# Three more output weights stored as halves in the tail of the first feed-forward, six units of the second set read from there

## The chip, the cores and the metric

The kernel runs on one core of one Trainium2 chip. The metric is the device time of one execution in microseconds. The kernel before takes 2192.62 us (median of 3 runs, 2192.11 to 2194.38). Five engines work side by side, each through its own instructions in a fixed order: PE (TensorE, matmuls), DVE (VectorE), ACT (ScalarE), POOL (GpSimd), and SP (SyncE), which here only issues DMAs.

## The reference

It is one inference step of a two-layer encoder trunk over 1056 tokens (1024 of a prompt and 32 of a sample) and 1024 channels, in float32. The part that the change touches is the second layer's attention and what frames it:

```
# layer 0: mLSTM mixer, then feed-forward;  layer 1: windowed attention, then feed-forward
x = layer_norm(ALPHA * x + mixer(x))
x = layer_norm(ALPHA * x + swiglu(x, w_gu[0], w_down[0]))          # first feed-forward
kv = x @ w_kv
q  = x @ w_q_b
o  = sink_attention(q, k, v, sinks, alibi)                         # 16 heads of 64
x  = layer_norm(ALPHA * x + o @ w_out_b)                           # w_out_b: 1024 x 1024
x  = layer_norm(ALPHA * x + swiglu(x, w_gu[1], w_down[1]))
```

## The kernel before

Activations lie transposed in SBUF: 8 tiles of 128 channels by 1056 tokens. The tokens are worked in quarters of 264 columns (in the projections for attention in groups of 384, 384 and 288). Every float32 product is made of three matmuls (`gemm`, L435 to L437): each operand is split in a high half `hi`, rounded to the format that the matmul takes, and a low half `lo = x - hi`; the three are hi·hi, hi·lo and lo·hi.

So each weight has to be split before use. A *unit* is a block of 128 output channels by 1024 input channels, and it is split in two *halves* f = 0 and 1 of 128 x 512 each. The class `Weights` does it in the order of use: SP loads the raw unit (512 KB) in a buffer `wr` (four of them), ACT (or POOL) casts it to `wh`, DVE or POOL subtracts to `wl` (L256 to L260). Five pairs `wh`/`wl` rotate, and some halves have a *home* of their own in memory that lies free at that time (`oh`, and `ex` of the next stage).

Some units are split ahead of time. While PE is busy with the first feed-forward, the task `split_before` loads half a unit at a time (`wraw`), casts it on ACT (`whi`, L1335), subtracts on DVE (L1337) and stores both results in a DRAM tensor `halves` (L1340). `BEFORE` lists these units: 2 of w_kv, 8 of w_q_b, and the first 3 (`EARLY`) of w_out_b, 26 halves in all. When `Weights` comes to such a unit, SP loads two blocks of 256 KB from `halves` (L253) in place of the raw load, cast and subtraction.

w_out_b is walked twice. The first set of its 8 units (118, 121, 124 and 125 to 129 in the program's count) makes the first quarter of columns, while attention still runs. The second set, units 130 to 137, makes quarters two to four, where each unit stays in memory until its third use. In the kernel before all of 130 to 137 are loaded raw and split on ACT and DVE; 132 to 137 go to homes in `ex`, memory that the attention's tiles leave free. When the first quarter is done, `finish` waits for the attention's last pieces, and the layer norm of each quarter (`ln_task`) runs on DVE, ACT and a few PE matmuls (L496, L513) beside the next quarter's matmuls.

Between attention and this product stands `mixed_parts`: it splits the attention's output (ACT, and DVE or POOL, L465 and L466) and then has SP load the residual input back from DRAM into the same place (`act<-scrx`, L1248). SP takes all DMAs in the order in which they were written, and so a DMA that waits holds those behind it.

The tail of the first feed-forward (`norm_tail` with `run`, L1657 on) multiplies its last eight weights (`dnt`) with the four quarters; the adds to `act` (L1662) are on DVE, with the layer norm of the quarter before.

Of the kernel before, what the change touches and what calls it, by code (L numbers as in the profile page):

```python
# [18 lines left out]
KT = D // P  # L19
# [10 lines left out]
LC = 64  # L30
WK = 3 * LC
EARLY = 3
D_FF = 2816
FT = D_FF // P

# [269 lines left out]
def kernel(ctx: ExitStack, tc: tile.TileContext, A, O):  # L305
    nc = tc.nc
    ctx.enter_context(tc.manual_schedule())
    wv = Weave()
# [3 lines left out]
    def pool(name, space=None, side=None):  # L312
        kw = {}
        if space is not None:
            kw["space"] = space
        if side is not None:
            kw["side"] = side
        return tc.tile_pool(name=name, bufs=1, reuse_waits="tile", **kw)

    def new(p, tag, shape, dt=F32, bufs=1):  # L320
        uid[0] += 1
        return p.tile(list(shape), dt, name=f"{tag}_{uid[0]}", tag=tag, bufs=bufs)
# [6 lines left out]
    units, on_vector, pairs = [], set(), set()  # L329

    def add(name, idx):
        units.append(A[name][idx] if idx is not None else A[name])
        return len(units) - 1
# [34 lines left out]
    U_KV, U_QB, U_OUT_B = [], [[], []], [[], []]  # L368
# [3 lines left out]
    for jp in range(QH // 4):  # L372
        U_QB[1] += [add("wqb", 2 * jp + i) for i in range(2)]
        if 0 < jp <= EARLY:
            U_OUT_B[0].append(add("wout_b", jp - 1))
    U_OUT_B[0] += [add("wout_b", u) for u in range(EARLY, 8)]
    U_OUT_B[1] += [add("wout_b", u) for u in range(8)]
# [1 line left out]
    on_vector.update((u, f) for u in U_O + U_OUT_A[0] for f in range(2))  # L379
    on_vector.update((u, f) for u in U_OUT_B[1][2:] for f in range(2))  # L380
    on_vector.update((u, f) for u in U_Q[:1] for f in range(2))
    on_vector.update((u, f) for u in U_OUT_B[1][:2] for f in range(2))
    on_vector.update((u, 0) for u in U_OUT_B[0][EARLY:])
    W = Weights(nc, base, units, pairs, on_vector, {(u, 1) for u in U_OUT_B[0][EARLY:]})
    BEFORE = [("wkv", i) for i in range(2)] + [("wqb", i) for i in range(8)] + [("wout_b", i) for i in range(EARLY)]
    for us in (*U_KV, *U_QB, U_OUT_B[0][:EARLY]):
        name = {2: "wkv", 8: "wqb", EARLY: "wout_b"}[len(us)]
        W.ready.update((u, BEFORE.index((name, i))) for i, u in enumerate(us))
    W.early = {up[i] for up in U_UP for i in range(FIRST, FT)}
    wv.feed = W.feed  # L390
# [23 lines left out]
    scr = dram.tile([P, KT, T], F32, name="scrx")  # L414
    W.halves = dram.tile([P, len(BEFORE), 2, 2, D // 2], F32, name="halves")
    OPS = ("x11", "x21", "t2", "t4", "t1", "t3", "x22")
# [136 lines left out]
    class LastNorm:  # L553
# [36 lines left out]
        def run(self):  # L590
            acc, sq = self.buf(0, 2), [self.buf(2 + 2 * i, 2) for i in range(3)]
            yield 1.2
            self.pc = self.bank()
            nc.tensor.matmul(self.pc, onesm[:], self.buf(10), start=True, stop=True)
            yield 0.6
            self.centre(3)
            self.centre(4, 2)
            self.centre(6, 2)
            self.centred = True
            yield 0.6  # L600
            self.centre(0, 2)
            nc.scalar.activation(sq[0], self.z(0, 2), AF.Square)
            self.centre(2)
            while self.i < 3:
                yield 0.3
            yield 0.6
            nc.scalar.activation(sq[1], self.z(2, 2), AF.Square)
            nc.gpsimd.tensor_add(acc, self.z(0, 2), self.z(2, 2))
            yield 1.0
            nc.vector.tensor_add(sq[0], sq[0], sq[1])  # L610
            while self.i < 5:
                yield 0.3
            yield 0.6
            nc.scalar.activation(sq[1], self.z(4, 2), AF.Square)
            nc.vector.tensor_add(acc, acc, self.z(4, 2))
            nc.vector.tensor_add(acc[:, 0], acc[:, 0], acc[:, 1])
            yield 1.4
            nc.vector.tensor_add(sq[0], sq[0], sq[1])
            nc.vector.tensor_add(sq[0][:, 0], sq[0][:, 0], sq[0][:, 1])
            while self.i < 6:  # L620
                yield 0.3
            nc.scalar.activation(sq[2][:, 0], self.z(6), AF.Square)
# [42 lines left out]
    def norm_tail(li, run, box, final=False):  # L665


        tasks = []
        for g, (cols, (c, zs)) in enumerate(QUARTERS):

            def after(order, i):
                if i in (3, 5, 7):
                    if i == 3 and g > 1:
                        wv.drain(tasks[g - 2])
                    acc = box[0].z[:, 0:2, c, zs]
                    pair = [ACT[:, order[j] : order[j] + 2, cols] for j in (i - 1, 0)]
                    nc.vector.tensor_add(acc, acc if i > 3 else pair[1], pair[0])
                if i == KT - 1:
                    nc.vector.tensor_add(acc[:, 0], acc[:, 0], acc[:, 1])

            if final and g == 3:
                wv.drain(tasks[1])
                run(g, cols, None, LastNorm(box[0].z, box[0].lnps, QUARTERS[g], li))
                break
            run(g, cols, after)
            if g == 0 and li & 1:
                nc.scalar.preload_act_table_set("natural_log_exp_and_others")
            last = g >= 3
            tasks.append(wv.launch(ln_task(box[0].z, box[0].lnps, QUARTERS[g], li, last, final)))
            box[0].norms = tasks  # L690
        return tasks
# [582 lines left out]
    def mixer_out(us, li, lx, opening=None, before=None, made=0):  # L1274

        box = [lx]

        def run(g, cols, after):
            if before:
                before(g)  # L1280
            if g == 3:
                lx = box[0]
                lx.sums = ExitStack()
                su = lx.sums.enter_context(pool("sums"))
                bufs = [new(su, f"su{i}", [P, 2, N4])[:] for i in range(2)]
                wv.drain(lx.norms[1])
                lx.comb = wv.launch(sums(lx, li, 0, bufs, 2.4))

            order = [6, 7, *range(6)] if g == 3 and not opening else list(range(KT))
            for i, m in enumerate(order):  # L1290
                if not g and m < made:
                    continue
                u = us[g > 0][m]
                W.get(u)
                if g < 2:
                    W.split_to(us[g][min(m + 2, KT - 1)])
                out_tile(u, m, cols)
                if g == 3 or u not in us[1]:
                    W.done(u)
                if g == 3 and (u, 0) in W.home:  # L1300
                    box[0].left += 1
                if box[0]:
                    after(order, i)
            if not box[0]:
                box[0] = opening()
                for i in range(KT):
                    after(order, i)

        return norm_tail(li, run, box), box[0]

    def split_before():

        ex = ExitStack()
        p = ex.enter_context(pool("before"))
        raws = [new(p, f"wraw{i}", [P, D // 2]) for i in range(2)]
        hi = new(p, "whi", [P, D // 2], F32R)
        todo = [(i, f) for i in range(len(BEFORE)) for f in range(2)]  # L1320

        def load(n):
            i, f = todo[n]
            name, idx = BEFORE[i]
            nc.sync.dma_start(raws[n % 2][:], A[name][idx][:, f * (D // 2) : (f + 1) * (D // 2)])

        load(0)
        yield 4.0
        for n, (i, f) in enumerate(todo):
            yield 3.0  # L1330
            if n + 1 < len(todo):
                load(n + 1)
            yield 2.0
            r = raws[n % 2][:]
            nc.scalar.copy(hi[:], r)  # L1335
            yield 1.5
            nc.vector.tensor_sub(r.bitcast(F32R), r, hi[:].bitcast(F32))  # L1337
            yield 1.8
            for k, t in enumerate((hi[:].bitcast(F32), r)):
                nc.sync.dma_start(W.halves[:, i, f, k, :], t)  # L1340
            W.stored.add((i, f))
            yield 3.7
        ex.close()

    def ffn(layer, li, tasks, lx, final):
# [26 lines left out]
        staging, splitting = [], []  # L1372
# [260 lines left out]
        for b in range(TAIL):  # L1633
# [8 lines left out]
            for j in range(2):  # L1642
                down(b, j)
            wv.drain(feeding.pop())
        for t in splitting:
            wv.drain(t)
        px.close()
        W.ahead = True
        dense_psum(5)
# [15 lines left out]
                    W.done(u)  # L1665

        r = norm_tail(li, run, [lx], final)
        lx.ex.close()
        return r

# [18 lines left out]
    n = D // 2  # L1689
# [353 lines left out]
    def before(g):  # L2043
        if g == 0:
            wv.drain(task, lambda: ast["placed"] >= last_item(7, 0))
        if g < 3:
            parts_made(g)
# [170 lines left out]
```

## Time and profile before

| | |
|---|---|
| runs | 2192.11, 2192.62, 2194.38 us |
| profiled execution, its own time | 2192.83 us |
| its span, first to last instruction | 2190.7 us |
| granted TensorE clock | 0.998 |
| PE busy | 2162.7 us (99%) |
| DVE, ACT, POOL busy | 1455.3, 991.9, 903.3 us |
| DMA | 322 MB, mean 147 GB/s |

What follows goes by microseconds from the span's start. The first feed-forward's tail is at about 1094 to 1164, attention with its projections at 1164 to 1406, the second set of output weights at 1406 to 1500. PE's busy time counts a matmul from its start to a modelled end, so that it says nearly always 99%; idle time is read from the waits and from the distance of one matmul's start to the next.

### The profile page before, as it was taken

What the parts mean: (1) busy time and instruction counts of PE and PEld (TensorE: products, weight loads), DVE (VectorE), ACT (ScalarE), POOL (GpSimd) and SP (SyncE); (2) the same over time, 40 slices, a digit from 0 to 9 for tenths busy, and PEclk for the clock granted to TensorE, in tenths of its full rate; (3) what the DMA queues carried; (4) which work ended last, traced back from release to release, by engine and by line L of the source; (5) the groups of instructions that cost most, each with busy time, mean ns of one, the idle gap of its engine ahead of it and who ended that gap; (6) DMA issues with size and microseconds to landing.
All of it is one profiled execution on the core that took longest, in us unless ns stands there. A gap on an engine that the chain in (4) does not pass through costs nothing.

```text
span 2190.7 us, 44028 instructions
## 1 busy us (share of the span) xinstructions
PE 2162.7 (99%) x16982; PEld 2136.5 (98%) x16982; DVE 1455.3 (66%) x2833; ACT 991.9 (45%) x2234; POOL 903.3 (41%) x926
## 2 busy tenths in 40 slices
PE   9999999999999999999999999999999999999997
PEld 9999999999999999999999999999999999999997
DVE  4465676778767666466657776888666666457657
ACT  4443355455444444322235777656444444422125
POOL 2544210003655655454421443501665655554441
PEclk9999999999999999999999999999999999999999
DMA  5221112212656555697517433511443433397712
GB/s 172 75 66 55 51 49 80 96 40 69 235 197 208 211 201 200 205 333 252 180 45 245 150 118 126 161 35 39 145 146 143 158 140 143 131 358 244 254 52 80
DMA packets 187361, 322.49 MB, mean 147 GB/s; under 512 B 18768, under 2 KB 124296, under 8 KB 187152
## 3 DMA queue, kind: packets, MB, share of 16 engines
q1 hardware_dynamic: 182800, 315.36, 43.1%
q10 hardware_dynamic: 4352, 4.33, 0.6%
q8 instruction: 134, 2.20, 0.4%
q14 instruction: 75, 0.61, 0.1%
HBM read 221.23 MB, written 96.57 MB: 145 GB/s over the span
## 4 chain that ended last, share of the span: by engine, by line
PE 86%; DVE 7%; ACT 3%; issue 1%; DMA 1%; POOL 0%; SPq 0%; DVEq 0%; ACTq 0%; POOLq 0%
PE d L435 10%; PE A L435 10%; PE A L437 10%; PE A L436 10%; PE d L437 10%; PE d L436 10%; PE B L435 7%; PE B L436 7%; PE B L437 7%; PE O L1986 1%; PE psS L1898 1%; PE T L1957 1%; DMA hs_x<-z 1%; ACT act L538 1%; PE T L988 1%
## 5 line engine op out<-in xcount | busy, mean ns | idle before, releaser
L260 POOL TENSOR_TENSOR wl_s<-wr,wh_s 128x512 fp32r<-128x512 f32 x224 | 304.2, 1367 | 241.2 <-ACT wh_s L258 181.4
L435 PE MATMUL d<-sx,wh 128*128 128x264 f32 (+2 forms) x1040 | 331.4, 319 | 0.2
L260 POOL TENSOR_TENSOR wl_a<-wr,wh_a 128x512 fp32r<-128x512 f32 x112 | 155.7, 1392 | 401.9 <-ACT wh_a L258 397.7
L437 PE MATMUL d<-sx,wl 128*128 128x264 f32 (+2 forms) x1040 | 316.2, 304 | 1.7 <-DVE wl L260 0.9
L436 PE MATMUL d<-sx,wh 128*128 128x264 f32 (+2 forms) x1040 | 315.7, 304 | 0.6 <-DVE sx L466 0.4
L435 PE MATMUL A<-sx,wh_s 128*128 128x264 f32 x896 | 254.5, 284 | 0.0
L436 PE MATMUL A<-sx,wh_s 128*128 128x264 f32 x896 | 254.2, 284 | 0.0
L437 PE MATMUL A<-sx,wl_s 128*128 128x264 f32 x896 | 254.0, 284 | 0.0
L258 ACT CAST wh_s<-wr 128x512 fp32r<-128x512 f32 x224 | 135.7, 618 | 192.1 <-DVE wr L201 102.9
L435 PEld LDWEIGHTS d<-sx,wh 128*128 128x128 f32 x1040 | 196.0, 188 | 3.6 <-ACT sx L465 0.4
L436 PEld LDWEIGHTS d<-sx,wh 128*128 128x128 f32 x1040 | 196.3, 189 | 1.9 <-DVE sx L466 1.1
L437 PEld LDWEIGHTS d<-sx,wl 128*128 128x128 f32 x1040 | 195.5, 188 | 2.4 <-DVE wl L260 1.4
L435 PE MATMUL d<-sx,ex 128*128 128x264 f32 x624 | 180.7, 290 | 0.1
L436 PE MATMUL d<-sx,ex 128*128 128x264 f32 x624 | 177.2, 284 | 0.0
L437 PE MATMUL d<-sx,ex 128*128 128x264 f32 x624 | 176.9, 284 | 0.0
L437 PEld LDWEIGHTS A<-sx,wl_s 128*128 128x128 f32 x896 | 168.8, 188 | 0.0
L435 PEld LDWEIGHTS A<-sx,wh_s 128*128 128x128 f32 x896 | 168.4, 188 | 0.2 <-issue 0.2
L436 PEld LDWEIGHTS A<-sx,wh_s 128*128 128x128 f32 x896 | 168.4, 188 | 0.0
L1396 POOL TENSOR_TENSOR z<-z 128x528 fp32r<-128x528 f32 x76 | 103.9, 1367 | 122.6 <-ACT z L1395 114.1
L435 PE MATMUL A<-ex,wh_s 128*128 128x264 f32 x448 | 127.5, 285 | 0.0
L436 PE MATMUL A<-ex,wh_s 128*128 128x264 f32 x448 | 127.1, 284 | 0.0
L437 PE MATMUL A<-ex,wl_s 128*128 128x264 f32 x448 | 127.1, 284 | 0.0
(377 smaller groups left out, 7126.6 us busy)
## 6 DMA issues: line engine op xcount, KB each, us to landing
wr<-in_gu SPq DMA_DIRECT2D x92, 512.0 KB, 4.4
hs_x<-z SPq DMA_DIRECT2D x72, 528.0 KB, 3.1
hs_t<-z SPq DMA_DIRECT2D x64, 528.0 KB, 4.7
sx<-hs_x SPq DMA_DIRECT2D x112, 264.0 KB, 5.9
sx<-hs_t SPq DMA_DIRECT2D x64, 264.0 KB, 6.1
ex<-hs_t SPq DMA_DIRECT2D x64, 264.0 KB, 6.0
wr<-in_dn SPq DMA_DIRECT2D x32, 512.0 KB, 4.9
wh<-halves SPq DMA_DIRECT2D x38, 256.0 KB, 3.2
```

What stands on the lines that cost most here:

```text
L258: self.nc.scalar.copy(hi, r)
L260: eng.tensor_sub(lo, r, hi.bitcast(F32))
L435: nc.tensor.matmul(out, ah, bh, start=start and k == 0, stop=False, **kw)
L436: nc.tensor.matmul(out, ah, bl, start=False, stop=False, **kw)
L437: nc.tensor.matmul(out, al, bh, start=False, stop=stop and k == last, **kw)
L538: nc.scalar.activation(z, z, AF.Identity, scale=gk, bias=bk)
L988: nc.tensor.matmul(pc[:, : 2 * (DV + 1)], keys, vt[j][:, c], start=True, stop=True)
L1396: eng.tensor_sub(lo.bitcast(F32R), buf(s), hi)
L1898: nc.tensor.matmul(ps[:rows, at : at + nk], lhs, k[:, k0 : k0 + nk], start=i == 0, stop=i == 1)
L1957: nc.tensor.transpose(pt[:nk, t, :rows], p[:rows, at : at + nk], ident[:rows, :rows])
L1986: nc.tensor.matmul(out, v[:nk], x, start=i == 0, stop=i == len(todo) - 1)
```

## The change

The list `BEFORE` grows by three units, so that w_out_b's units 0 to 5 are stored (32 halves in all). The first 26 halves are made when they were. The last six wait until the tail of the feed-forward begins, and then follow each other at 7.2 in place of 12 us of the program's own clock; the task is drained behind the tail instead of ahead of it. Of the second set, units 130 to 135 are then loaded from `halves`; 136 and 137 are still split. In the first quarter of that set (the call with `opening`, g = 1) the loads run up to 5 units ahead, in place of 2.

```diff
+FRONT, AFTER = 13, 3
...
-    on_vector.update((u, f) for u in U_OUT_B[1][:2] for f in range(2))
...
-    BEFORE = [("wkv", i) for i in range(2)] + [("wqb", i) for i in range(8)] + [("wout_b", i) for i in range(EARLY)]
-    for us in (*U_KV, *U_QB, U_OUT_B[0][:EARLY]):
-        name = {2: "wkv", 8: "wqb", EARLY: "wout_b"}[len(us)]
+    BEFORE = [("wkv", i) for i in range(2)] + [("wqb", i) for i in range(8)] + [("wout_b", i) for i in range(EARLY + AFTER)]
+    for us in (*U_KV, *U_QB, U_OUT_B[0][:EARLY], U_OUT_B[1][: EARLY + AFTER]):
+        name = {2: "wkv", 8: "wqb"}.get(len(us), "wout_b")
...
-                    W.split_to(us[g][min(m + 2, KT - 1)])
+                    W.split_to(us[g][min(m + (2 if opening is None or not g else 5), KT - 1)])
...
+    tail_begun = []
...
         for n, (i, f) in enumerate(todo):
-            yield 3.0
+            if n < 2 * FRONT:
+                pauses = 3.0, 2.0, 1.5, 1.8, 3.7
+            else:
+                pauses = 1.4, 1.2, 1.4, 1.6, 1.6
+                while not tail_begun:
+                    yield 0.5
+            yield pauses[0]
             if n + 1 < len(todo):
                 load(n + 1)
-            yield 2.0
+            yield pauses[1]
...
-        for t in splitting:
-            wv.drain(t)
+        tail_begun.append(True)
         px.close()
...
         r = norm_tail(li, run, [lx], final)
+        for t in splitting:
+            wv.drain(t)
         lx.ex.close()
```

PE's instructions and POOL's stand in the same order as before. Three places of the other engines matter.

SP at the turn from attention to the second set, before. `wr130` to `wr137` are the raw units, `act<-scrx` the residual input coming back:

```order
L1248 DMA act_75<-scrx_77 128x4x384
L172 DMA wr130_17095<-in_wout_b 128x1024
L172 DMA wr131_17105<-in_wout_b 128x1024
L172 DMA wr132_17275<-in_wout_b 128x1024
L172 DMA wr133_17285<-in_wout_b 128x1024
L1248 DMA act_75<-scrx_77 128x4x288
L172 DMA wr134_17426<-in_wout_b 128x1024
L1248 DMA act_75<-scrx_77 128x4x384
L1248 DMA act_75<-scrx_77 128x4x288
L172 DMA wr135_17549<-in_wout_b 128x1024
L172 DMA wr136_17555<-in_wout_b 128x1024
L172 DMA wr137_17587<-in_wout_b 128x1024
```

SP at the same place now, from the last two `act<-scrx` on. `wh131_1` and `wl131_1` are the second half of unit 131; the four rows `ex ... x4` are units 132, 133, 134 and 135, each with two halves of two blocks:

```order
L1248 DMA act_75<-scrx_77 128x4x384
L1248 DMA act_75<-scrx_77 128x4x288
L254 DMA wh131_1_17565<-halves_78 128x512
L254 DMA wl131_1_17566<-halves_78 128x512
L254 DMA ex_1326_17553<-halves_78 128x512 x4
L173 DMA wr136_17573<-in_wout_b 128x1024
L254 DMA ex_1326_17553<-halves_78 128x512 x4
L173 DMA wr137_17579<-in_wout_b 128x1024
L254 DMA ex_1326_17553<-halves_78 128x512 x4
L173 DMA wr138_17585<-in_gu 128x1024
L254 DMA ex_1326_17553<-halves_78 128x512 x4
L173 DMA wr139_17591<-in_gu 128x1024
```

Before, five raw units stood ahead of the last two `act<-scrx`; now three halves (130 whole, 131's first) do, and 18 blocks of 256 KB with four raw units between them stand behind.

DVE in the first quarter of the second set, before (`L1272` adds a finished block to `act` and frees its bank in PSUM):

```order
L679 TENSOR_TENSOR z_1327_17537<-z_1327_17537 128x264
L260 TENSOR_TENSOR wl131_1_17546<-wr131_17105,wh131_1_17545 128x512
L260 TENSOR_TENSOR ex_1326_17533<-wr132_17275,ex_1326_17533 128x512 x2
L260 TENSOR_TENSOR ex_1326_17533<-wr133_17285,ex_1326_17533 128x512
L1272 SCALAR_TENSOR_TENSOR act_75<-act_75,d_1328_17557 128x264
L260 TENSOR_TENSOR ex_1326_17533<-wr133_17285,ex_1326_17533 128x512
L260 TENSOR_TENSOR ex_1326_17533<-wr134_17426,ex_1326_17533 128x512 x2
L1272 SCALAR_TENSOR_TENSOR act_75<-act_75,d_1329_17589 128x264
```

And now:

```order
L679 TENSOR_TENSOR z_1327_17557<-z_1327_17557 128x264
L261 TENSOR_TENSOR ex_1326_17553<-wr136_17573,ex_1326_17553 128x512
L1272 SCALAR_TENSOR_TENSOR act_75<-act_75,d_1328_17593 128x264
L261 TENSOR_TENSOR ex_1326_17553<-wr136_17573,ex_1326_17553 128x512
L261 TENSOR_TENSOR ex_1326_17553<-wr137_17579,ex_1326_17553 128x512 x2
L1272 SCALAR_TENSOR_TENSOR act_75<-act_75,d_1329_17625 128x264
L261 TENSOR_TENSOR wl138_0_17674<-wr138_17585,wh138_0_17673 128x512
L1272 SCALAR_TENSOR_TENSOR act_75<-act_75,d_1330_17657 128x264
```

The splits of 131 to 135 are gone, and those of 136, 137 and 138 (the next feed-forward's first unit) stand ahead of the first three adds.

DVE in the tail of the first feed-forward, at the layer norm of its second quarter, now. Before, the row of `wraw1` isn't there:

```order
L501 TENSOR_TENSOR act_75<-ln_860_13712,act_75 128x2x264
L1669 TENSOR_TENSOR act_75<-act_75,d_859_13708 128x264
L550 TENSOR_TENSOR sx_76<-act_75,sx_76 128x2x264
L501 TENSOR_TENSOR act_75<-ln_860_13712,act_75 128x2x264 x2
L1345 TENSOR_TENSOR wraw1_696_6664<-wraw1_696_6664,whi_697_6665 128x512
L1669 TENSOR_TENSOR act_75<-act_75,d_861_13742 128x264
L677 TENSOR_TENSOR z_627_4632<-act_75 128x2x264
L501 TENSOR_TENSOR act_75<-ln_860_13712,act_75 128x2x264
```

The last of the six added subtractions has come into the chain of that norm; the other five stand in the same way between the tail's adds.

More of the change, by code (lines that the diff above doesn't have):

```diff
@@ L1329, in split_before @@
         for n, (i, f) in enumerate(todo):
-            yield 3.0
+            if n < 2 * FRONT:
[5 more added lines that the diff above has]
+            yield pauses[0]
             if n + 1 < len(todo):
                 load(n + 1)
-            yield 2.0
+            yield pauses[1]
             r = raws[n % 2][:]
             nc.scalar.copy(hi[:], r)
-            yield 1.5
+            yield pauses[2]
             nc.vector.tensor_sub(r.bitcast(F32R), r, hi[:].bitcast(F32))
-            yield 1.8
+            yield pauses[3]
             for k, t in enumerate((hi[:].bitcast(F32), r)):
@@ L1341, in split_before @@
             W.stored.add((i, f))
-            yield 3.7
+            yield pauses[4]
         ex.close()
```

## Prediction

> **What bounds the kernel now.** I read the page first, then PE's matmuls per stretch, then PE's waits, then the engines around the one wait that the change touches.
>
> ```profile
> span 2190.7 us, 44028 instructions
> PE 2162.7 (99%) x16982; PEld 2136.5 (98%) x16982; DVE 1455.3 (66%) x2833; ACT 991.9 (45%) x2234; POOL 903.3 (41%) x926
> ...
> 1520.00:1540.00 20.00, 20.00 (x167) 20.00 (x166) 17.15 (x19) 9.54 (x19) 12.44 (x8) 1.00 0.19 55
> ...
> 1380.00:1390.00 10.00, 10.00 (x88) 10.00 (x86) 9.45 (x33) 8.21 (x27) 9.03 (x11) 1.00 0.63 184
> 1390.00:1400.00 10.00, 9.02 (x78) 8.80 (x76) 9.32 (x24) 7.55 (x21) 9.41 (x10) 1.00 0.44 121
> ...
> 1410.00:1420.00 10.00, 9.10 (x74) 8.82 (x73) 9.31 (x18) 3.64 (x7) 0.00 (x0) 1.00 0.95 311
> ```
>
> (Columns of a stretch: length; busy time and instructions of PE, weight load, DVE, ACT, POOL; clock; DMA share, GB/s.) PE is the bound. In undisturbed feed-forward 167 matmuls touch 20.00 us, two of them only at its edges: one starts every 0.121 us. Those 264-column matmuls set the pace after attention too: an output block is 24 of them, 2.91 us; half a unit of weights lasts 1.45 us. PE's order does not change, so only its waits can. Those in reach:
>
> ```profile
> PE T L1957 <- POOL s L1932: 1.0, 1, 1.0
> PE d L437 <- DVE wl L260: 0.9, 1, 0.9
> ...
> 1410.36 0.28 PE L435 MATMUL d<-sx,wh 128*128 128x264 f32 x1
> 1410.48 0.28 PE L436 MATMUL d<-sx,wh 128*128 128x264 f32 x1
> 1411.66 0.39 PE L437 MATMUL d<-sx,wl 128*128 128x264 f32 x1 [0.90 <-DVE wl L260]
> ```
>
> The second wait is that of unit 131's second half: PE wants its first matmul at 1410.36, and the third, the first with `wl`, starts at 1411.66 and not 1410.60: 1.06 us late. What it waits for:
>
> ```profile
> 1407.69 0.61 ACT L258 CAST wh<-wr 128x512 fp32r<-128x512 f32 x1
> ...
> 1408.60 1.94 DVE L677 TENSOR_TENSOR z<-z,act 128x528 f32<-128x528 f32 x2
> 1410.57 0.43 DVE L679 TENSOR_TENSOR z<-z 128x264 f32<-128x264 f32 x1
> 1410.92 0.68 DVE L260 TENSOR_TENSOR wl<-wr,wh 128x512 fp32r<-128x512 f32 x1
> ...
> 1431.15 0.43 DVE L1272 SCALAR_TENSOR_TENSOR act<-act,d 128x264 f32<-128x264 f32 x1 [2.33 <-PE d L437]
> ```
>
> The raw data were there; the subtraction stood behind the norm's sums on DVE. After it the quarter runs through: its last block's add starts at 1431.15, released by PE, so the quarter ends at about 1430.9. That is also 1411.66 + 154 matmuls x 0.121 + 0.5 for two norm matmuls.
>
> **What goes.** Twelve halves of 130 to 135 are no longer split here:
>
> ```profile
> L260 DVE TENSOR_TENSOR ex<-wr,ex 128x512 fp32r<-128x512 f32 x12 | 7.8, 686 | 0.7 <-ACT ex L258 0.7
> L260 DVE TENSOR_TENSOR wl<-wr,wh 128x512 fp32r<-128x512 f32 x7 | 6.3, 899 | 1.1 <-ACT wh L258 1.1
> ...
> L258 ACT CAST ex<-wr 128x512 fp32r<-128x512 f32 x12 | 6.7, 615 | 4.9 <-DMA wr<-in_wout_b 4.9
> L258 ACT CAST wh<-wr 128x512 fp32r<-128x512 f32 x7 | 4.3, 615 | 0.0
> ```
>
> Four `wh`/`wl` and eight `ex`: 12 x 0.615 = 7.4 us of ACT, and 4 x 0.9 + 8 x 0.69 = 9.1 us of DVE. All of it lay beside PE except the 1.06 us above. Before 1406 DVE has 9.32 of 10 us busy, so a little of PE's small gaps may close. The wait of 1.0 us on POOL stays: POOL's order is the same, and its chain (two splits of 128 and 129, then the scale) keeps its length; at most it gets faster where no subtraction runs beside it. I take -0.5 us, from 0 to -1.0.
>
> **What is added at the turn.** 24 blocks of 256 KB replace six raw loads. The first six (130, and 131's first half) go in the time of five raw loads that left, and have until 1406 and 1408.9: hidden by attention. The other 18 stand on SP behind the last two `act<-scrx`:
>
> ```profile
> 1397.99 0.38 SPq L1248 DMA_DIRECT2D act<-scrx  x1
> ...
> 1406.56 3.08 SPq L1248 DMA_DIRECT2D act<-scrx  x2
> ...
> SPq L1248 <- POOL sx L466: 4.5, 3, 2.4
> ...
> 1407.87 1.36 POOL L466 TENSOR_TENSOR sx<-act,sx 128x288 fp32r<-128x288 f32 x1 [1.34 <-ACT sx L465]
> ```
>
> The two are issued from 1406.56 to 1409.64; the second waits for POOL's last subtraction (1407.87 + 1.36 = 1409.23), which hangs on attention's end and does not move. So `wh131_1` can be issued at 1409.7 at the earliest, 0.7 us before PE wants it. And the DMA engines are full then:
>
> ```profile
> 1407.50:1410.00 2.50, 2.50 (x23) 2.50 (x23) 2.43 (x4) 2.50 (x6) 1.36 (x1) 1.00 0.81 251
> 1410.00:1412.50 2.50, 1.60 (x13) 1.39 (x12) 2.46 (x5) 1.43 (x3) 0.00 (x0) 1.00 0.94 292
> 1413.50:1419.00 5.50, 5.50 (x46) 5.43 (x45) 4.84 (x10) 1.76 (x3) 0.00 (x0) 1.00 0.99 363
> ...
> 1171.00:1176.00 5.00, 5.00 (x30) 4.93 (x29) 3.75 (x7) 2.94 (x5) 0.00 (x0) 1.00 0.96 311
> 1183.00:1197.00 14.00, 14.00 (x81) 14.00 (x80) 10.77 (x18) 11.29 (x22) 4.74 (x4) 1.00 1.04 360
> ...
> GB/s 307 360 389 349 369 380 345 357 258 240 290 312 341 378 389 398 393 384 414 388 414 419 378 421 404 373 396 383 378 408 358 340 297 251 364 365 307 334 381 387
> ...
> wh<-halves SPq DMA_DIRECT2D x38, 256.0 KB, 3.2
> ```
>
> The first three rows are the residual inputs (786 and 590 KB, until about 1412.5) and the raw loads of before. The next two are stretches in which stored halves are loaded with the engines full (share 0.96, 1.04): 311 and 360 GB/s. The last row but one is the second of these in forty slices. I take 345 GB/s, nearer to the longer stretch: half a unit (two blocks, 524 KB) takes 1.52 us, and so does a raw unit. With DMAs served in their order, the queue behind 1412.5 is: 131's second half, 132, raw 136, 133, raw 137, 134, raw 138, 135. Its second half of 135 is the twelfth piece of 524 KB. A piece counts as landed some 0.5 us after its last packet (a lone 256 KB block lands at 3.2, of which 0.76 is transfer at that rate and most of the rest lies ahead of the packets).
>
> - 131's second half: 1412.5 + 1.52 + 0.5 = 1414.5. PE has waited since 1410.4.
> - From there a unit and the raw one beside it take 3 x 1.52 = 4.6 us of DMA, and PE eats a unit in 2.9. So PE waits again, some 1.6 us ahead of each of 133, 134 and 135.
> - 135's second half: 1412.5 + 12 x 1.52 + 0.5 = 1431.2. PE then has 12 + 48 matmuls left: 7.3 us, end of the quarter at 1438.5.
>
> Against 1430.9 that is **+7.6 us**, the 1.06 us won being in it. With 363 GB/s (1.44 us a piece) it is +6.6, with 311 (1.69 us) +9.7. DVE's new order costs nothing more: the first adds wait behind the splits of 136 (lands 1419), 137 (1423.6) and 138 (1428.2), but their banks are wanted only by blocks 4, 5 and 6, at 1425, 1429.7 and 1432.7. If the raw loads came 3 us later this cover would be gone for 138.
>
> The Trainium skill (DMA: Bandwidth & Descriptors, Where 436 GB/s comes from) has two ceilings: 435 GB/s for the fabric, and about 358 per core for loads from HBM, of which it says that the second binds here. By 358 the sum would be +6.8, by 435 some +4. The rows above (360, 363) stand on the side of the first of these, and leave single slices of 421 for the other.
>
> **What is added in the tail.** Six casts and six subtractions, 18 DMAs (6 loads, 12 stores):
>
> ```profile
> 1094.00:1164.00 70.00, 70.00 (x568) 69.67 (x567) 42.48 (x78) 26.81 (x50) 19.30 (x18) 1.00 0.26 86
> ...
> L1335 ACT CAST whi<-wraw x26: 602/622/624, 542.7 to 863.8; 128x512 fp32r<-128x512 f32 x26
> L1337 DVE TENSOR_TENSOR wraw<-wraw,whi x26: 675/745/1794, 544.2 to 869.5; 128x512 fp32r<-128x512 f32 x26
> ...
> 1146.66 0.43 DVE L508 TENSOR_TENSOR z<-z 128x264 f32<-128x264 f32 x1
> ...
> 1147.97 0.61 PE L513 MATMUL ln<-z,onesm 128*128 128x264 f32 x2
> ...
> 1079.54 17.44 SPq L172 DMA_DIRECT2D wr<-in_dnt  x6
> 1097.07 0.38 SPq L253 DMA_DIRECT2D wh<-halves  x1
> ...
> 1111.69 0.43 DVE L1662 TENSOR_TENSOR act<-act,d 128x264 f32<-128x264 f32 x1 [1.76 <-PE d L437]
> ```
>
> 6 x 0.62 = 3.7 us of ACT and 6 x 0.75 = 4.5 us of DVE, beside 70 us of PE, which is busy for all of them (first row), with DVE at 42 and ACT at 27 us. Only the last subtraction meets a tight place: the second quarter's norm ends its sum at 1147.09 and PE takes it at 1147.97, 0.88 us of room, against 0.62 + 0.75 of added work in that chain: about 0.5 us, from 0 to 1. On SP the stores wait for DVE, and the tail's last raw unit (issued last of the six, until 1096.98) now stands behind the first of them, which can go after DVE's second add and a subtraction, at some 1100; that unit's block is the eighth, added at 1111.69 and so begun by PE at about 1109.3, with a landing and a split of some 6 us between: it holds. The first block of `halves` (1097.07) is for the projections behind 1164. I take +0.3.
>
> **Sum:** +7.6 - 0.5 + 0.3 = +7.4 us. The profiled execution took 2192.8 us (span 2190.7 and 2.1 around it), which makes 2200.2; the median of the runs is 0.2 below it, so 2200.0, or 0.34% slower. 0.2% of the time, 4.4 us, is about what a measurement can tell from no change: it lies at 2197.0.
>
> **Rivals.**
>
> 1. *Not slower: the relief decides.* The 1.06 us at 1411.66 and the 1.0 us at 1396 go, and the blocks land in time: -2.0, 2190.6. It needs 131's second half by 1410.6, thus issued ahead of the `act<-scrx`, and a unit with its raw neighbour (1.57 MB) in 2.9 us, 540 GB/s. For it: ACT and DVE do lose 16 us of work. Against it: SP's order, and no row above 421 GB/s. It decides from 540 GB/s on. Chance 0.12, for what I may have misread in what SP waits for.
> 2. *Late, but faster DMA.* At 420 GB/s, as the best slices have, a piece takes 1.25 us: 135 lands at 1428.0, the quarter ends at 1435.3, +4.4; with the other terms 2196.9. The fabric figure of the page named above would end here. Against it: no stretch of 5 us has over 363. Chance 0.14.
> 3. *Slower than I say.* At 311 GB/s, +9.7, with the tail's full 1 us and no relief: 2203.3; and if the split of 138 on DVE then holds the norm of the first quarter up against PE's L513 behind the quarter, 1 to 2 us more, 2205. Chance 0.12.
>
> My forecast has 0.62: 2198 to 2203.
>
> **How the numbers follow.** The range leaves out rival 1 and the far end of 3: 2196.0 to 2205.0. Slower by over 0.2% (above 2197.0): 0.62 and 0.12 and half of rival 2, less 0.03: 0.78. Faster by over 0.2% would take 4.4 us, twice what the waits in reach hold: 0.04. The same: 0.18.
>
> **What would show it.** In the profile after, PE's waits have new rows at L437 or L435 ended by a DMA from `halves`, the first of about 4 us near 1414, then three of 1 to 2 us; the DMA share is near 1 from 1407 to 1431; the first block's add (L1272) comes after 1419; the tail shows at most one wait of PE on L513 below 1 us. I am wrong if PE's first `wl131_1` matmul starts by 1412, or if after it no wait for `ex` is seen: then DMA is faster, or its order another, than I hold.

## The result, and the profile after

| | changed kernel | kernel before |
|---|---|---|
| median | 2197.95 us (11 runs, 2197.57 to 2199.13) | 2192.27 us (11 runs, 2192.09 to 2194.38) |
| ratio | 1.0024, 95% interval 1.0016 to 1.0032 | |
| profiled execution | 2197.57 us, span 2195.0 | 2192.83 us, span 2190.7 |

It is slower by 5.7 us (3.5 to 7.0 by the interval); the forecast was 2200.0.

```profile
span 2195.0 us, 44074 instructions
PE 2165.2 (99%) x16982; PEld 2139.6 (97%) x16982; DVE 1451.0 (66%) x2827; ACT 990.3 (45%) x2228; POOL 905.5 (41%) x926
```

DVE and ACT are hardly less busy: of the twelve halves that the second set no longer splits, six are split in the tail instead. PE's waits between 1130 and 1445, so from the tail to behind the turn:

```profile
PE d L435 <- DMA wh<-halves: 3.2, 1, 3.2
...
PE T L1966 <- POOL s L1941: 0.5, 1, 0.5
PE ln L513 <- DVE z L508: 0.2, 1, 0.2
```

One new wait on `halves`, not four; the wait on POOL is half as long; the wait on the subtraction of 131 is gone. Around the new wait, PE's matmuls one by one, then the stretches behind it (columns as in the prediction):

```profile
1409.20 0.28 PE L437 MATMUL d<-sx,wl 128*128 128x264 f32 x1
1412.70 0.59 PE L435 MATMUL d<-sx,wh 128*128 128x264 f32 x1 [3.22 <-DMA wh<-halves]
...
1418.42 0.42 PE L435 MATMUL d<-sx,ex 128*128 128x264 f32 x1
1418.64 0.42 PE L436 MATMUL d<-sx,ex 128*128 128x264 f32 x1
...
1419.21 0.28 PE L436 MATMUL d<-sx,ex 128*128 128x264 f32 x1
1419.33 0.28 PE L437 MATMUL d<-sx,ex 128*128 128x264 f32 x1
```

```profile
1409.50:1412.20 2.70, 0.00 (x0) 0.00 (x0) 0.43 (x1) 0.00 (x0) 0.00 (x0) 1.00 1.01 333
1412.30:1419.00 6.70, 6.30 (x27) 6.09 (x28) 0.66 (x2) 1.14 (x2) 0.00 (x0) 0.50 1.04 399
1419.10:1424.00 4.90, 4.90 (x40) 4.83 (x40) 2.51 (x5) 1.15 (x2) 0.00 (x0) 1.00 1.05 406
```

The first row: PE has no matmul. The second: behind the wait the granted clock is 0.50 for 6.8 us, and a matmul starts every 0.220 us (1418.42 to 1418.64) and not every 0.121. The third: clock 1.00 again (1419.21 to 1419.33). The DMA engines are full all the while (share 1.01 to 1.05), behind the wait at about 400 GB/s.

Why 131's second half comes late shows on SP, in the order of its issues:

```profile
1405.52 3.06 SPq L1248 DMA_DIRECT2D act<-scrx  x2
1408.68 0.46 SPq L254 DMA_DIRECT2D wh<-halves  x1
1409.23 0.38 SPq L254 DMA_DIRECT2D wl<-halves  x1
1409.70 1.80 SPq L254 DMA_DIRECT2D ex<-halves  x4
```

The two blocks stand behind both residual loads, as forecast, and are issued when PE is about to want them.

**A finer measure.** The kernels here are alike in their first 36 us, and still their executions lie up to 1.6 us apart at its end, so small differences drown in the span. But PE has the same matmuls in the same order in all of them (the idle ones that runs 1 and 6 add are left out of the count), so each start can be set against that of the same matmul before, and a place's cost is the change of this shift across it. "Turn" is the shift's change from 1390 to 1445, "tail" from 1136 to 1165, both against the kernel before; "median" is the difference of the medians, good to some 2 us. A shift comes from one execution of each kernel.

| kernel | turn | tail | median | ratio, 95% |
|---|---|---|---|---|
| changed | +4.80 | +0.44 | +5.68 | 1.0016 to 1.0032 |
| 1: idle matmuls in the wait | +5.18 | +0.40 | +7.03 | 1.0017 to 1.0040 |
| 2: one residual load later | +2.81 | +0.39 | +3.78 | 1.0008 to 1.0025 |
| 3: 131 split as before | +3.96 | +0.39 | +3.66 | 1.0007 to 1.0025 |
| 4: the tail's part alone | 0.00 | +0.45 | +0.30 | 0.9991 to 1.0009 |
| 5: raw 136, 137 early | +4.93 | +0.39 | +5.71 | 1.0016 to 1.0034 |
| 6: both 5 and 1 | +3.18 | +0.38 | +4.83 | 1.0012 to 1.0030 |
| 7: both residual loads later | +0.01 | +0.39 | +1.01 | 0.9995 to 1.0013 |
| 8: both 7 and 5 | -0.86 | +0.38 | -0.05 | 0.9991 to 1.0009 |
| 9: all 32 halves in the body | +5.00 | 0.00 | +11.36 | 1.0036 to 1.0063 |
| 10: 8 and 9 | -1.08 | 0.00 | +5.11 | 1.0014 to 1.0032 |
| 11: 8, 30 halves in the body | -1.07 | +0.01 | +0.85 | 0.9996 to 1.0014 |
| 12: 8, 28 halves in the body | -1.14 | 0.00 | -1.12 | 0.9987 to 1.0005 |

The changed kernel's 4.80 at the turn add up: 3.38 of wait (1409.20 to 1412.70, less a pace of 0.12), some 30 matmuls that start 0.10 us further apart, 3.0, less the old wait of 1.06 and 0.70 of relief between 1390 and 1409; 4.6.

### The profile page after: what moved, and what is told of

Its sections match the earlier page's. It is cut to its first block, busy times and chain, and to the rows that moved or that the text cites. A ratio compares the mean times of both kernels' runs of the same rounds, so it can differ in the third digit from the quotient of the medians.

```text
span 2195.0 us, 44074 instructions
## 1 busy us (share of the span) xinstructions
PE 2165.2 (99%) x16982; PEld 2139.6 (97%) x16982; DVE 1451.0 (66%) x2827; ACT 990.3 (45%) x2228; POOL 905.5 (41%) x926
## 5 line engine op out<-in xcount | busy, mean ns | idle before, releaser
L261 POOL TENSOR_TENSOR wl_a<-wr,wh_a 128x512 fp32r<-128x512 f32 x112 | 155.4, 1390 | 407.4 <-ACT wh_a L259 403.3
```

The costliest lines, as they stand in the source:

```text
L261: eng.tensor_sub(lo, r, hi.bitcast(F32))
```

## The experiments

The wait and the slow clock together could be the whole loss (theory A below). Or the prediction's bound, the stream of stored halves, is there all the same, and the slow PE only came no earlier than its weights (theory B).

**1. Keep PE busy while it waits.**

```diff
+        if warm:
+            d = new(lx.lnps, "ln", [P, 512], bufs=2)
+            gemm(ps, w[:4], x[:4], part=0)
+            for _ in range(warm):
+                nc.tensor.matmul(d[:, :P], onesm[:], onesm[:], start=True, stop=True)
+            gemm(ps, w[4:], x[4:], part=1)
...
+                out_tile(u, m, cols, 14 if opening and g == 1 and m == 1 else 0, box[0])
```

`warm` is 14 for unit 131 in the first quarter of the second set and 0 elsewhere; `part` lets the two calls of `gemm` add up in one block.

> The changed kernel with 14 idle matmuls (128x128 of ones into a bank of the norm that is not read) put between the two halves of unit 131 in the second quarter, so that PE is busy during some 3.0 of the 3.5 us in which it waits for the second half; nothing else differs. Theory A (one late half, and the clock at half speed behind it, are the whole loss): the clock stays at 1.0 behind the wait, 30 matmuls start every 0.121 us instead of 0.220, -3.1 us, 2194.9. Theory B (the loads of 133 to 135 are the bound, as the prediction had it, and the slow clock only hid that): the waits come out ahead of 133, 134 and 135, about 1 us each, and only some 0.9 us is won, 2197.1.

The clock stayed up, and nothing was won: 2199.19 us, turn +5.18 where the changed kernel has +4.80. PE's matmuls that waited, and the stretch that had been slow:

```profile
1415.16 0.39 PE L437 MATMUL d<-sx,wl 128*128 128x264 f32 x1 [0.50 <-DMA wl<-halves]
1420.74 0.39 PE L437 MATMUL d<-sx,ex 128*128 128x264 f32 x1 [0.17 <-DMA ex<-halves]
1424.09 0.36 PE L435 MATMUL d<-sx,ex 128*128 128x264 f32 x1 [0.40 <-DMA ex<-halves]
1428.01 0.36 PE L435 MATMUL d<-sx,ex 128*128 128x264 f32 x1 [0.39 <-DMA ex<-halves]
...
1413.70:1420.50 6.80, 6.14 (x43) 5.18 (x42) 0.33 (x1) 0.98 (x2) 0.00 (x0) 1.00 1.04 397
```

43 matmuls in 6.8 us where 27 had been in 6.7, and then waits ahead of 133, 134 and 135. From 134's first matmul to 135's it is 3.92 us where PE needs 2.91: that is three pieces of 524 KB at 401 GB/s, two halves of a unit and the raw one beside them. Theory A falls. Theory B's waits are there, 1.0 us from one of these units to the next (3.92 less 2.91), but its time, 2197.1, was missed by 2.1. Of that the turn has 1.3: not even the 0.9 us that it granted the slow clock was to be had. The rest is no more than what one place gives that this edit doesn't touch: between 940 and 960 the shift grew by 1.2 here, and by -0.3 to +1.2 among the kernels that are alike there.

**2. One residual load later.** The load (rows 4 to 7, last columns) is kept as a closure (a function that is called later) and issued in the second quarter of columns, behind the weights.

```diff
+                elif k == 7 and src is scr and g in (2,):
+                    held.append(lambda ...: nc.sync.dma_start(act_g[g][:, 4:8], src[:, 4:8, ...]))
...
+                while opening and g == 1 and m == 0 and held:
+                    held.pop(0)()
                 out_tile(u, m, cols)
```

> The changed kernel with the last load of the residual input (rows 4 to 7 of the last 288 columns, 590 KB) issued behind the weights of 132 to 135 instead of ahead of 131's second half. 131's second half is issued up to 2.7 us earlier and has 1.5 us less ahead of it: PE waits 0.5 to 1.6 us at 1409 instead of 3.5, too short for the clock to drop. Theory A: 2 to 3 us of wait and 3.1 us of slow clock go, 2192.4 (2191.9 to 2193.0). Theory B: the loads of 133 to 135 bound the quarter at 400 GB/s, PE waits some 1 us ahead of each, 2194.8.

**3. 131 split as before.**

```diff
-        W.ready.update((u, ...) for i, u in enumerate(us))
+        W.ready.update((u, ...) for i, u in enumerate(us) if u != U_OUT_B[1][1])
```

> The changed kernel with unit 131 split on ACT and DVE as before, the other five units (130, 132 to 135) from the stored halves; the tail stores as many halves as in the changed kernel. Theory A: no late half and no slow clock, the old wait of about 1 us on the subtraction of 131 is back: 2192.6 (before, +0.4 of the tail, less a little relief). Theory B: the other stored halves still come late, three waits of about 1 us ahead of 133, 134 and 135: 2195.0.

Both end about 1 us above theory B's time and more than 3 above theory A's: 2195.94 and 2195.82 us. PE's waits of the second run, then of the third:

```profile
1412.05 0.39 PE L435 MATMUL d<-sx,wh 128*128 128x264 f32 x1 [1.38 <-DMA wh<-halves]
...
1421.45 0.36 PE L435 MATMUL d<-sx,ex 128*128 128x264 f32 x1 [0.39 <-DMA ex<-halves]
1425.38 0.36 PE L435 MATMUL d<-sx,ex 128*128 128x264 f32 x1 [0.40 <-DMA ex<-halves]
```

```profile
1410.91 0.39 PE L437 MATMUL d<-sx,wl 128*128 128x264 f32 x1 [0.87 <-DVE wl L261]
1413.01 0.39 PE L435 MATMUL d<-sx,ex 128*128 128x264 f32 x1 [0.61 <-DMA ex<-halves]
1414.16 0.39 PE L437 MATMUL d<-sx,ex 128*128 128x264 f32 x1 [0.65 <-DMA ex<-halves]
...
1421.46 0.36 PE L435 MATMUL d<-sx,ex 128*128 128x264 f32 x1 [0.45 <-DMA ex<-halves]
1425.39 0.36 PE L435 MATMUL d<-sx,ex 128*128 128x264 f32 x1 [0.41 <-DMA ex<-halves]
```

With no late half of 131 at all (third), the next ones are late, and 134 to 135 takes 3.93 us again. The stream is a bound, whoever waits first.

**4. The tail alone.** The list of `ready` without the second set, so that 130 to 137 are all split as before, and `split_to` at 2 units again.

> The kernel before, with only the six more halves split and stored in the tail of the first feed-forward; the second set of output weights takes none of them. Both theories: only the second quarter's norm in the tail is 0.4 us later: 2192.7 (2192.2 to 2193.0). Rival C (the tail or what stands behind it carries a good part of the loss, on SP or in the halves loaded for the projections): 2194 or more.

2192.46 us; the shift steps by 0.45 between 1136 and 1165, and by nothing at the turn. Rival C is out.

**5 and 6. Are there two bounds side by side?** If the stream and the slow PE each give nearly the whole loss, easing one gives nothing, and easing both gives much. Raw 136 and 137 are loaded early, into idle time of the DMA engines, alone and with the idle matmuls:

```diff
         self.parts[key] = (hi, lo)
         self.njob += 1
+        if key == self.hook:
+            self.load_to(u + 6)
...
+    W.hook = (U_OUT_B[1][1], 0)
```

`hook` is unit 131's first half.

> The changed kernel with the raw loads of units 136 and 137 (two pieces of 524 KB) issued right behind 131's first half, into the 3 us in which the DMA engines stood idle ahead of the residual loads, instead of among the stored halves of 132 to 134. The stream behind 131's second half gets 2.6 us shorter. Theory C (two bounds side by side: the stream of stored halves, and PE at half clock behind the 3.2 us wait, each of which gives nearly the whole loss alone): the wait and the slow stretch stay, and about nothing is won, 2197.8 (2197.0 to 2198.3). Theory D (the stream alone is the bound, the slow clock costs nothing): 2195.8.

> The raw loads of 136 and 137 early as in the run beside it, and the 14 idle matmuls in the wait for 131's second half as in the first run. Theory C: with both bounds eased the waits ahead of 134 and 135 go and the clock stays up: 2.0 us under the changed kernel, 2196.0. Theory D: the same as with the early loads alone. Were both the idle matmuls and the early loads worth nothing, 2198 to 2199.

The stretch behind the wait, in the fifth run and in the sixth:

```profile
1413.50:1420.20 6.70, 5.93 (x26) 5.76 (x27) 0.65 (x2) 0.00 (x0) 0.00 (x0) 0.50 1.05 396
```

```profile
1413.50:1420.20 6.70, 5.37 (x41) 5.08 (x41) 0.53 (x2) 0.00 (x0) 0.00 (x0) 1.00 1.05 392
```

At the turn: changed +4.80, idle matmuls +5.18, early loads +4.93, both +3.18. Neither alone gains, the two together 1.6 of the 2.0 us that theory C gave (C as these two expectations have it: two bounds side by side). The medians (2197.47, 2196.59) point the same way, though their difference alone is within the 2 us that medians can tell.

**7 and 8. Take the queue away.** Both residual loads later (the second run's edit with `g in (1, 2)`), and the same with raw 136 and 137 early.

> The changed kernel with both last loads of the residual input (786 and 590 KB, 3.4 us at 400 GB/s) issued behind the weights of 132 to 135. 131's second half is issued at some 1406 and lands before PE wants it at 1409.2: no wait there, no slow clock. By the stream at 400 GB/s PE still waits 0.4, 1.0 and 1.0 us ahead of 133, 134 and 135: the quarter ends 4.5 us earlier than in the changed kernel, 2193.4 (2192.8 to 2194.5). If the stream were no bound, 2191.

> Both residual loads late and the raw loads of 136 and 137 early: the stream of stored halves starts some 3.4 us earlier and is 2.6 us shorter, so each half lands before PE wants it. No wait of PE on a DMA is left at the turn, the old wait on the subtraction of 131 is gone too: 2.0 us less than the kernel before at the turn, 0.4 us more in the tail, 2190.6 (2190.0 to 2192.0), so the fastest of all. If the splits of 136 and 137 or the residual input then come too late, 2193.

SP's issues in the seventh, then in the eighth:

```profile
1403.85 0.32 SPq L254 DMA_DIRECT2D wh<-halves  x1
1404.26 0.38 SPq L254 DMA_DIRECT2D wl<-halves  x1
```

```profile
1401.00 0.95 SPq L173 DMA_DIRECT2D wr<-in_wout_b  x2
1402.52 0.33 SPq L254 DMA_DIRECT2D wh<-halves  x1
```

131's second half is issued at 1403.85 and 1402.52 in place of 1408.68; as these executions run 1.7 and 0.4 us behind the changed one there, it is 6.6 us earlier in both. In the seventh, 2192.77 us, no wait for it is left, only those of the stream:

```profile
1419.21 0.36 PE L435 MATMUL d<-sx,ex 128*128 128x264 f32 x1 [0.22 <-DMA ex<-halves]
1423.15 0.36 PE L435 MATMUL d<-sx,ex 128*128 128x264 f32 x1 [0.40 <-DMA ex<-halves]
```

In the eighth, 2191.71 us, these are gone too, but for 0.3 us, and the turn is 0.86 shorter than before, not the 2.0 that I expected. I had counted the old wait of 1.06 as all gain. From 1405 to the quarter's end PE's matmuls before lose 1.7 us in gaps longer than the pace of 0.122, that wait among them, and here 1.5, in ten gaps of 0.1 to 0.4. By the shift, 0.73 of the 0.86 lie ahead of 1405, so what remains is nearly all the relief there.

**9 to 12. The tail's 0.44 us.** All halves in the body of the feed-forward (`FRONT, AFTER = 16, 3`), alone and with the edits of the eighth run.

> The changed kernel with all 32 halves split and stored in the body of the first feed-forward at the old pace (12 us apiece, the last at some 940 us) and none in its tail. If the tail's 0.44 us (PE one matmul of the second quarter's norm later) is what the six halves cost, it goes and nothing comes in its place, since PE is the bound there: 2197.5, by the records a shift of -0.4 us at 1165. If the six halves cost PE something in the body as well (DVE 42 of 70 us busy in the tail, more in the body), the shift comes back between 860 and 940.

> All three together: both residual loads late, the raw loads of 136 and 137 early, and all halves stored in the body. By the records the turn is 0.85 us shorter than in the kernel before (as in the run with the first two) and the tail no longer: 2191.0 against 2191.8 (2190.3 to 2191.8), too little for the measurement of one call to tell for certain; it shows in the shift of PE's start times at 1165 (0 against the kernel before, not +0.44) and at 1445 (-0.85).

The tail's step went (0.00), and more than ten times as much came in the body: between 940 and 960 PE's shift grew by 8.2 and 5.4 us, 2203.25 and 2197.00 us. In the ninth run PE and ACT there:

```profile
949.57 0.36 PE L435 MATMUL A<-sx,wh_s 128*128 128x264 f32 x1 [3.33 <-ACT wh_b L259]
...
947.48 0.63 ACT L1403 CAST z<-z 128x528 fp32r<-128x528 f32 x1 [2.89 <-DMA hs_x<-z]
948.02 0.61 ACT L259 CAST wh_a<-wr 128x512 fp32r<-128x512 f32 x1
948.54 0.61 ACT L259 CAST wh_b<-wr 128x512 fp32r<-128x512 f32 x1
```

A store of `hs_x` ends late, the cast of `z` behind it comes at 947.48 (943.76 in the changed kernel), and PE's weights are cast behind that. On SP the stores of the 31st half are issued at 937.68 and 938.49, between two stores of `hs_x`. They can't be all that holds `hs_x` up, for the one ahead of them is late already (935.54, in the changed kernel 933.03); the one behind them is 3.9 us late (940.65 for 936.78). Ahead of both stands the load of the 32nd half, at 930.22. Which of these pieces costs how much isn't shown. So fewer in the body, with the edits of the eighth run:

> The kernel with both residual loads late, raw 136 and 137 early and the halves stored in the body, but only 30 of the 32 in the body (the last at some 918 us) and two in the tail. If the 5.2 us that PE lost near 950 with all 32 in the body came from the last one or two halves alone, whose casts and stores fell among the block change at 938 to 950 (the cast of z on ACT at 947.46 instead of 943.76), it is gone: shift at 960 back at 0 to 0.3 against the changed kernel, 2191.5. If the body is too full for any of the six, about 2 to 3 us of it stays: 2194.

> As the run before it, with 28 halves in the body (the last at some 892 us, clear of the block change at 938) and four in the tail. The turn is 1.0 us shorter than in the kernel before; the body costs nothing (shift between 940 and 960 within 0.3); the tail 0 to 0.44 us, since only the last subtractions meet the second quarter's norm. By the records 0.6 to 1.0 us less than the kernel before, 2191.2 if that one stands at 2192.0; the timing of one call, good to some 2 us, can't tell it from no change. If 1.3 us stay near 950 with 28 too, the halves in the body are not what costs there.

With 30 the shift between 940 and 960 grew by 1.8, with 28 by -0.4, in a place that scatters from -0.3 to +1.2 anyway: the last two halves cost most of it, and whether the two ahead of them cost anything isn't settled. Four halves in the tail already cost nothing there, so its 0.44 came with the last two. The twelfth is the fastest of all, 2191.09 us against 2192.21 (ratio 0.9996, 0.9987 to 1.0005): by the shift 1.1 us better at the turn, by the timing not to be told from the kernel before. So with every place mended the change is worth about nothing that the timing can show.

## Why the prediction was right, and where its steps failed

- **Sign and size.** Forecast +7.4, measured +5.2 by the shift (turn and tail), +5.7 by the medians. 2197.95 lies in the range, but 0.05 us below the forecast's own 2198 to 2203.
- **131's second half behind the residual loads: right.** Forecast was a landing at 1414.5 and 4.1 us of wait; on the clock of before (the changed execution runs 1.04 us ahead there) PE starts at 1413.7, after 3.4 us. Runs 2, 7 and 8 show the cause: 1.4 and no wait with one and two residual loads moved.
- **The stream at 345 GB/s: mis-sized, by a misreading of its own row.** A piece takes 1.31 us, not 1.52. The changed kernel at 1412 to 1428:

```profile
DMA packets 2997, 6.43 MB, mean 402 GB/s; under 512 B 333, under 2 KB 333, under 8 KB 2997
...
q1 hardware_dynamic: 2997, 6.43, 104.8%
```

  The stretch before that I leaned on, 1183 to 1197, then the five microseconds 1187 to 1192 out of it, then 1413.5 to 1419:

```profile
DMA packets 3393, 5.04 MB, mean 360 GB/s; under 512 B 308, under 2 KB 1609, under 8 KB 3392
...
q10 hardware_dynamic: 1368, 1.36, 28.1%
...
1187.00:1192.00 5.00, 5.00 (x31) 5.00 (x30) 4.26 (x6) 2.65 (x6) 2.42 (x2) 1.00 1.05 391
DMA packets 1335, 1.96 MB, mean 391 GB/s; under 512 B 119, under 2 KB 659, under 8 KB 1335
...
q10 hardware_dynamic: 572, 0.57, 32.2%
...
DMA packets 545, 2.00 MB, mean 363 GB/s; under 512 B 57, under 2 KB 57, under 8 KB 545
```

  My argument against rival 2, that no stretch of 5 us has over 363, is wrong by the prediction's own forty slices: from 1187 on the stretch had 391 for 5 us. The second queue (q10, ACT's stores of `scrx`) and the small packets, nearly half of all, don't explain the mean of 360, for the fast middle holds as much of both; and 1413.5 to 1419 had one queue, few small packets, and 363 all the same. What sets these rates apart stays open. With 1.31 us the prediction's own sum ends 135 at 1428.7 and the quarter at 1436.0: +5.1, with its other two terms +4.9, against 5.2 by the shift. So rival 2, faster DMA, describes the run best. The Trainium skill (DMA: Bandwidth & Descriptors, Where 436 GB/s comes from) says that about 358 GB/s per core binds loads from HBM; 402 over 16 us on one core is above that, so its other figure, the fabric's 435, is the nearer ceiling here.
- **Three waits of 1.6 us ahead of 133 to 135: the rows are absent, the bound is not.** By the text's own mark ("if no wait for `ex` is seen") DMA would have had to be faster or in another order. It is faster, but at 1.0 us each the waits would still have shown. They don't because PE ran at half clock and used its weights up no sooner than they came; runs 1 to 3 bring them out.
- **The clock: not foreseen.** I summed the 4 us wait without asking what follows it. It did no harm only because the stream was the bound beside it, and that was luck; with the stream eased (run 5 against 6) the slow stretch costs 1.75 us.
- **What goes, -0.5: measured -0.70** between 1390 and 1409, POOL's wait 0.5 in place of 1.0 among it. Run 4 has none of this (0.02), so it comes from the splits that are gone. **The tail, +0.3: measured +0.44**, at the place named, the second quarter's norm.
- **Rival 1** needed 131's second half issued ahead of the residual loads; run 8 made that so and shows what was to be had: about -0.5 in all (turn -0.86, tail +0.38), not -2.0.

## What to carry to other kernels

Trading splits on engines off the critical path for twice the bytes is a loss where the DMA queue is the next bound: count the pieces in the queue between the first consumer and the last, and look for the rate in the fast parts of full stretches too, not only in their means. When one late transfer is mended and the time doesn't move, look for a second bound of nearly the same length; it takes an experiment with both eased to see it. And a place in the middle of PE-bound work isn't free for side work: here the last two of 32 halves cost PE some 4 to 6 us (5.4 and 8.2 less 1.8) where they fell on a block change.

## What the runs showed of the hardware that I had not expected

Waits of 3.22 us (changed kernel) and 3.79 us (run 5) were followed by 6.8 us at a granted clock of 0.50; waits of 1.38 us (run 2) and 1.14 us (run 6) by none. But length alone doesn't decide. In run 9 two waits stood near each other; in run 10 the first of them came at the same place:

```profile
949.57 0.36 PE L435 MATMUL A<-sx,wh_s 128*128 128x264 f32 x1 [3.33 <-ACT wh_b L259]
955.59 0.56 PE L435 MATMUL A<-sx,wh_a 128*128 128x264 f32 x1 [2.87 <-DVE act L1608]
...
949.60:952.40 2.80, 2.80 (x23) 2.80 (x24) 2.80 (x4) 0.00 (x0) 1.62 (x2) 1.00 1.03 417
955.00:961.00 6.00, 5.41 (x24) 5.44 (x25) 3.05 (x5) 1.14 (x2) 2.52 (x2) 0.50 1.07 388
```

```profile
949.55 0.53 PE L438 MATMUL A<-sx,wh_s 128*128 128x264 f32 x1 [3.20 <-ACT wh_b L259]
...
949.60:953.00 3.40, 3.40 (x16) 3.40 (x17) 3.40 (x5) 0.00 (x0) 1.60 (x2) 0.50 1.02 408
953.10:955.00 1.90, 1.13 (x10) 0.92 (x8) 1.90 (x4) 0.00 (x0) 0.00 (x0) 1.00 1.09 372
```

In run 9 the clock is 1.00 behind the longer wait and 0.50 behind the shorter; in run 10 it is 0.50 behind 3.20 us, for 3.4 us. The Trainium skill (TensorE: Matmul & The Clock Gate, What's actually happening) says that the clock halves after at least one idle window of some 3.4 us, that the window runs freely, and that the clock comes back after some 3.4 us of work. That nearly the same idle time can go either way agrees with a free-running window; a drop behind 2.87 us doesn't agree with a whole window of idle time. The slow stretches agree with a whole window of work: in run 10 PE worked from the start of its 3.4 us, while in the changed kernel PE still idled in the first 0.4 us of the 6.8 (1412.3 to 1412.70), so that only the second 3.4 us were full.
